# A two-layer hybrid decoder trunk on one core: products of seven blocks in both FFNs, and the order at the FFN's end

## The chip, the cores and the metric

One NeuronCore of a Trainium2 chip runs the whole program in one launch. The metric is device time in microseconds. The engines are called PE (TensorE; PEld is its weight load), DVE (VectorE), ACT (ScalarE), POOL (GpSimd) and SP (SyncE, which here only issues DMAs). DMAs are issued by SP and by POOL.

## The reference

Two layers, each a mixer and an FFN with a sandwich norm around both. The FFN is what the change is about:

```python
def ffn_sublayer(h, pre_g, post_g, w_up, conv_w, w_down):
    u = rms_norm(h, pre_g)
    z = jnp.einsum("bld,df->blf", u, w_up)          # 1024 -> 2 * 2816
    z = causal_depthwise_conv(z, conv_w)            # 3 taps
    g, up = jnp.split(z, 2, axis=-1)
    y = jnp.einsum("blf,fd->bld", jax.nn.silu(g) * up, w_down)
    return h + rms_norm(y, post_g)
```

The mixer before it joins forgetting attention (8 heads), a conv module and a short gated conv behind one input projection, norms each head and projects out. The sequence is 512 tokens and 16 meta tokens, L = 528, float32.

## The kernel before

**Precision and tiling.** Activations lie as [128 features, 528 positions] tiles. Each float32 matmul is made of three fp32r matmuls on split operands (hi x hi, hi x lo, lo x hi; `mm3`, L786). A weight chunk is loaded by SP as `raw`, rounded by ACT to `whi`, and DVE subtracts to get `wlo`. In the FFN's main loop that is `prep_one` (L591, L592 for the parts of a pair of seven; L601, L602 for whole chunks); in the stages with an order written out by hand it is `plan_block` (loads L734, ACT L738, DVE L742). `next_w` keeps two weights ahead.

**The FFN.** `w_up` has 22 gate blocks and 22 up blocks of 128 columns; pair f is gate block f and up block f. They run in three parts of 8, 7 and 7 pairs. After each part eight blocks of `w_down` are multiplied with that part's gated values: in parts 0 and 1 in the main loop, summed into `yp` (L2351, L2353), in part 2 in `finish` together with the post norm and the first products of what follows. `ffn_gate` (L2117 on) makes the gated values of a pair: three conv taps each for gate and up (ACT L2120, DVE L2122), silu (ACT L2132), the product (DVE L2136), and its split into `y` (ACT L2139, DVE L2140), which the down products read.

**Products of seven.** In layer 1 (`SEVEN_IN = (1,)`) twelve of the 22 pairs (`SEVEN`) are not made as 2 x 8 x 3 x 2 matmuls but as seven block products over half of the features and half of the positions, 7 x 4 x 3 matmuls (`seven_pair`, `product`, L2234). They need four differences of u blocks, which `normalised` builds during part 0 (DVE and ACT, in the gaps of pairs 2 to 6 and during the down products), and three parts of weights beside the gate chunk: two halves `c` and `b` of a sum of gate and up blocks, and half of the up chunk, `d`. Parts `b` are split into the tiles `shi` and `slo` (one buffer each), `d` into `y7`. During these parts h lies in DRAM (`h_dram`), and its tile serves as four more `raw` buffers.

**Weight sums.** The sum for a pair is made in DRAM ahead of its use (`sum_steps`, L525): three copies issued by SP (L537 to L539), then three accumulating DMAs issued by POOL (L533). `SUMS = {1: (8, 4)}` puts eight of layer 1's sums into layer 0's FFN and four into mixer 1. In an FFN one step is taken at each `tick`, once a pair and once a down block: POOL copies one column of a fresh result (L2152) and the step is issued behind it. In a mixer the steps are queued in the planner at the lowest urgency, one sum each `SUM_EVERY` us, each add due `SUM_LAT` us after the step before it.

**Stored splits.** During layer 0's down products, `store_one` (L610) splits six of mixer 1's weight chunks ahead (L615, L616) into `whi`/`wlo` of a pool of five buffers and POOL writes them to DRAM (L619), from where mixer 1 fetches them ready.

**Order.** Mixers, `finish` and the first products run under an order written out by a planner (`Flow`, `tc.manual_schedule`), with costs and due times given in the code; the FFN's main loop is ordered by the tile framework. `tc.issue_after(x)` makes what is issued inside come behind x on x's engine. In `finish`, `products` runs the first two down blocks with all but the last gated pair first, because the last one arrives late:

```python
for group in (ks[:-1], ks[-1:]):
    for h in range(2):
        for i in range(2):
```

so the accumulator of the first half takes k = 0 to 5 at once (f = 15 to 20 in part 2), and only f = 21 is left for the end. ACT loads the table set for the norms behind the last silu (L2135).

Of the kernel before, what the change touches and what calls it, by code (L numbers as in the profile page):

```python
# [10 lines left out]
F32 = mybir.dt.float32  # L11
F32R = mybir.dt.float32r
BF16 = mybir.dt.bfloat16
AF = mybir.ActivationFunctionType
ALU = mybir.AluOpType

P = 128
# [10 lines left out]
NF = DFF // P  # L28
# [3 lines left out]
SEVEN = (8, 9, 10, 11, 12, 13, 15, 16, 17, 18, 19, 20)  # L32
SEVEN_IN = (1,)
SUMS = {1: (8, 4)}
SUM_US, SUM_LAT, SUM_EVERY = 0.9, 5.0, 40.0
K2 = KD // 2
# [352 lines left out]
def tile_hybrid_trunk(ctx: ExitStack, tc: tile.TileContext, xT, wflat, pv_d, out):  # L389
# [135 lines left out]
    def sum_steps(l, f):  # L525

        gate, up = (flat_w(up_chunk[l, t]) for t in (f, NF + f))
        t = sums[l, f] = T(dram, [P, 4, SB], F32, f"w_sum{l}_{f}")
        n, o = P * 2 * SB, offs[up_chunk[l, f]]
        diag = wflat[o:o + 2 * (n + SB)].rearrange("(e q) -> e q", e=2)[:, :n].rearrange("e (p s) -> p e s", p=P)[:, :, :SB]  # L530

        def put(to, src):
            nc.gpsimd.dma_start(to, src, accum_op=ALU.add)  # L533

        def copies():
            with tc.issue_after(last_load[0].ins):
                nc.sync.dma_start(t[:, 0], up[:, :SB])  # L537
                nc.sync.dma_start(t[:, 1], up[:, :SB])
                nc.sync.dma_start(t[:, 2:4], gate.rearrange("p (e s) -> p e s", e=2))  # L539

        return copies, lambda: put(t[:, 0:2], diag), lambda: put(t[:, 2], t[:, 1]), lambda: put(t[:, 3], t[:, 2])

# [67 lines left out]
    def store_one():  # L610

        if fetched:
            i, sz, raw = fetched.popleft()
            hi, lo = (T(wx[0], [P, WCHUNK], F32R, t) if sz <= WCHUNK else T(wp, [P, CHUNK], F32R, t) for t in ("whi", "wlo"))
            nc.scalar.copy(hi[:, :sz], raw[:, :sz])  # L615
# [1192 lines left out]
    def finish(norms, h, h_at, spans, ks, rhs, y_at, yp, gpost, gpre, nsplit, first=None, rz=None, scaled=None,  # L1808
# [45 lines left out]
        def products():  # L1854

            m1 = KD - nsplit
            for m0, z in [(m, m + 2) for m in range(0, m1, 2)] + [(m1, KD)]:
                for hf in range(2):
# [4 lines left out]
                    if m0 == 0:  # L1863
# [6 lines left out]
                        t = [mmt(x.buf) for x in slots]  # L1870
                        for group in (ks[:-1], ks[-1:]):
                            for h in range(2):
# [170 lines left out]
    for l in range(DEPTH):  # L2043
# [23 lines left out]
        with tc.tile_pool(name=f"fp{l}", bufs=2, reuse_waits="tile") as fp:  # L2067
# [57 lines left out]
            def ffn_gate(f):  # L2125

                cs = []
                for e, t in enumerate((f, NF + f)):
                    c = T(fp, [P, 2, H], F32, "c", 4).rearrange("p a b -> p (a b)")[:, :2 * fw]
                    gate_conv(t, zs[(2 * f + e) % len(zs)], c)  # L2130
                    cs.append(c)
                silu = nc.scalar.activation(cs[0], cs[0], AF.Silu)  # L2132
                if f == NF - 1:
                    with tc.issue_after(silu.ins):
                        nc.scalar.preload_act_table_set(EXPSET)  # L2135
                mul_ins[0] = nc.vector.tensor_mul(cs[0], cs[0], cs[1])  # L2136
                slot = next(f - sum(PARTS[:p]) for p in range(len(PARTS)) if f < sum(PARTS[:p + 1]))
                ghi, glo = (t[:, :2 * fw] for t in y_pair(slot))
                nc.scalar.copy(ghi, cs[0])  # L2139
                glo_ins[0] = nc.vector.tensor_sub(glo, cs[0], ghi.bitcast(F32))  # L2140
# [5 lines left out]
            seven = SEVEN if l in SEVEN_IN else ()  # L2146
            todo = deque(step for to, place in ((l + 1, 0), (l, 2)) for f in sums_at(to, place) for step in sum_steps(to, f))

# [65 lines left out]

            mul_ins, glo_ins = [None], [None]
            ts, n_seven, primed = [], [0], set()
# [74 lines left out]
            for part, nf in enumerate(PARTS):  # L2291
# [65 lines left out]
                else:  # L2357
# [7 lines left out]
                    if not final:  # L2365
# [3 lines left out]
                        first = First(lambda b, k, hf, raw=raw: raw[hf][b][k] if raw[hf] else u_rhs(b, k, hf), [H, H], {})  # L2369
                    with tc.manual_schedule(engines=every):  # L2370
                        plan_begins()
                        norms.factors([rs, zs[0][:, 2:]], h=APART)
                        flow.yields = YE
                        if not final:
                            plan_w(after_down, WE)
                        plan_w(len(chunks) if final else after_mixer[l + 1])
                        t_last = [Tok(flow.now + 7.5)]
                        finish(norms, h, {}, o_spans, ks, grhs, lambda k, nf=nf: t_last if k == nf - 1 else [], yp,
                               gains("ffn_post_g"), gpre, SPLIT["ffn_w_down"], first, raw=raw, rzs=rzs, u_at=u_at)
# [52 lines left out]
```

## Time and profile before

| what | value |
|---|---|
| median of three runs | 1286.39 us (1286.29 to 1289.18) |
| profiled execution | 1285.76 us |
| its span, first to last instruction | 1283.8 us |
| mean granted PE clock | 0.996 |
| DMA moved, mean rate | 176.30 MB, 137 GB/s |
| mixer 0, FFN 0 (about) | 32 to 276 us, 276 to 635 us |
| mixer 1, FFN 1 (about) | 673 to 915 us, 915 to 1284 us |

How to read the profile: an engine's share is its busy time over the span. The chain of waits is followed back from the last instruction to what released each step, so its shares say which engine's work set the end. A window's row gives a stretch, its length, each engine's busy time (and instructions), the granted PE clock, the share of the 16 DMA engines and GB/s. A timeline's row gives start, duration, engine, line, what it writes and reads, and in brackets how long the engine was idle and what ended that. `x2` merges two in a row.

### The profile page before, as it was taken

What the parts mean: (1) busy time and instruction counts of PE and PEld (TensorE: products, weight loads), DVE (VectorE), ACT (ScalarE), POOL (GpSimd) and SP (SyncE); (2) the same over time, 40 slices, a digit from 0 to 9 for tenths busy, and PEclk for the clock granted to TensorE, in tenths of its full rate; (3) what the DMA queues carried; (4) which work ended last, traced back from release to release, by engine and by line L of the source; (5) the groups of instructions that cost most, each with busy time, mean ns of one, the idle gap of its engine ahead of it and who ended that gap; (6) DMA issues with size and microseconds to landing.
All of it is one profiled execution on the core that took longest, in us unless ns stands there. A gap on an engine that the chain in (4) does not pass through costs nothing.

```text
span 1283.8 us, 24209 instructions
## 1 busy us (share of the span) xinstructions
PE 1261.4 (98%) x9660; PEld 1209.3 (94%) x9660; DVE 889.3 (69%) x1505; ACT 666.9 (52%) x1273; POOL 155.1 (12%) x333
## 2 busy tenths in 40 slices
PE   8999999999999999999999999999999999999987
PEld 8999899999999999999999998999999799989987
DVE  7888765688634764566578887756799648747854
ACT  7254577564333432244573545766555457527643
POOL 1313311001122112100003234110000000000000
PEclk9999999999999999999999999999999999999989
DMA  7136132605579638732552585555134235344511
GB/s 241 34 102 160 51 101 91 224 18 149 150 230 265 168 95 243 190 105 75 172 218 63 155 192 116 137 130 181 73 120 140 92 122 181 115 140 141 199 50 67
DMA packets 69393, 176.30 MB, mean 137 GB/s; under 512 B 7632, under 2 KB 18000, under 8 KB 69024
## 3 DMA queue, kind: packets, MB, share of 16 engines
q1 hardware_dynamic: 60784, 155.74, 38.0%
q0 software_dynamic: 8496, 19.01, 8.4%
q8 instruction: 76, 1.25, 0.4%
q14 instruction: 37, 0.30, 0.1%
HBM read 151.09 MB, written 37.95 MB: 147 GB/s over the span
## 4 chain that ended last, share of the span: by engine, by line
PE 91%; DVE 4%; ACT 2%; DMA 1%; issue 1%; POOL 0%; SPq 0%; DVEq 0%; ACTq 0%
PE psum L786 68%; PE psum L2234 9%; PE psum L1356 4%; PE psum L1620 3%; PE psum L1586 2%; PE psum L923 1%; DMA raw<-in_w_dram 1%; PE psum L1542 1%; PE psum L1686 1%; PE psum L1272 1%; ACT whi L738 1%; DVE c L2122 0%; DVE wlo L742 0%; DVE yp L999 0%; POOL dm L1557 0%
## 5 line engine op out<-in xcount | busy, mean ns | idle before, releaser
L786 PE MATMUL psum<-y,whi 128*128 128x264 f32 (+3 forms) x1968 | 386.8, 300 | 7.2 <-ACT y L2139 3.7
L786 PE MATMUL psum<-uhi,whi 128*128 128x264 f32 (+1 forms) x1456 | 349.8, 288 | 1.7 <-ACT uhi L2018 0.7
L786 PE MATMUL psum<-ulo,whi 128*128 128x264 f32 (+1 forms) x1456 | 343.3, 284 | 0.6 <-DVE ulo L2020 0.4
L786 PE MATMUL psum<-uhi,wlo 128*128 128x264 f32 (+1 forms) x1456 | 342.5, 284 | 0.0
L786 PEld LDWEIGHTS psum<-y,whi 128*128 128x128 f32 x1968 | 306.5, 189 | 22.1 <-ACT y L2139 4.3
L786 PE MATMUL psum<-y,wlo 128*128 128x264 f32 (+3 forms) x984 | 273.7, 298 | 1.1 <-DVE wlo L742 1.1
L786 PEld LDWEIGHTS psum<-uhi,whi 128*128 128x128 f32 x1456 | 245.9, 188 | 6.2 <-issue 2.0
L786 PEld LDWEIGHTS psum<-ulo,whi 128*128 128x128 f32 x1456 | 246.0, 188 | 1.3 <-DVE ulo L2020 0.6
L786 PEld LDWEIGHTS psum<-uhi,wlo 128*128 128x128 f32 x1456 | 245.5, 188 | 0.0
L786 PEld LDWEIGHTS psum<-y,wlo 128*128 128x128 f32 x984 | 178.1, 189 | 6.7 <-DVE wlo L742 1.5
L601 ACT CAST whi<-raw 128x1024 fp32r<-128x1024 f32 (+1 forms) x80 | 82.2, 1029 | 116.3 <-PE psum L786 84.2
L2122 DVE SCALAR_TENSOR_TENSOR c<-zs,pv,c 128x528 f32<-128x528 f32 (+1 forms) x176 | 131.1, 756 | 10.1 <-ACT c L2120 8.1
L602 DVE TENSOR_TENSOR wlo<-raw,whi 128x1024 fp32r<-128x1024 f32 (+1 forms) x80 | 95.7, 1198 | 41.4 <-ACT whi L601 40.6
L742 DVE TENSOR_TENSOR wlo<-raw,whi 128x1024 fp32r<-128x1024 f32 (+2 forms) x80 | 95.5, 1203 | 30.2 <-ACT whi L738 29.7
L738 ACT CAST whi<-raw 128x1024 fp32r<-128x1024 f32 (+2 forms) x80 | 81.8, 1030 | 27.5 <-PE psum L786 20.2
L1102 DVE SCALAR_TENSOR_TENSOR cacc<-apad,pv,cacc 128x528 f32<-128x528 f32 x120 | 87.7, 772 | 0.1
L2139 ACT CAST y<-c 128x528 fp32r<-128x528 f32 (+1 forms) x44 | 27.5, 626 | 73.0 <-DVE c L2136 72.9
L2120 ACT ACTIVATE c<-zs,pv 128x528 f32<-128x528 f32 (+1 forms) x88 | 63.2, 727 | 3.2 <-DVE zs L2272 1.5
L2085 DVE TENSOR_TENSOR zs<-psum,rz 128x528 f32<-128x528 f32 x40 | 28.3, 708 | 51.4 <-PE psum L786 50.5
L1620 PE MATMUL psum<-pf,vals 128*128 128x400 f32 (+3 forms) x160 | 50.7, 399 | 0.6 <-POOL pf L1600 0.6
L1586 PE MATMUL psum<-q,k 128*128 128x128 f32 (+2 forms) x192 | 51.2, 348 | 0.0
L2132 ACT ACTIVATE c<-c 128x528 f32<-128x528 f32 (+1 forms) x44 | 28.1, 640 | 44.3 <-DVE c L2122 44.3
(265 smaller groups left out, 1974.3 us busy)
## 6 DMA issues: line engine op xcount, KB each, us to landing
raw<-in_w_dram SPq DMA_DIRECT2D x135, 512.0 KB, 4.2
raw<-in_w_dram SPq DMA_DIRECT2D x27, 448.0 KB, 4.2
h<-w_sum SPq DMA_DIRECT2D x14, 512.0 KB, 4.1
h<-in_w_dram SPq DMA_DIRECT2D x13, 512.0 KB, 3.7
w_sum<-in_w_dram SPq DMA_DIRECT2D x24, 256.0 KB, 8.9
w_sum<-in_w_dram SPq DMA_DIRECT2D x12, 512.0 KB, 6.9
w_sum<-in_w_dram POOLq DMA_DIRECT2D x12, 512.0 KB, 7.6
w_sum<-w_sum POOLq DMA_DIRECT2D x24, 256.0 KB, 5.4
```

The source lines that it names most:

```text
L601: nc.scalar.copy(hi[:, :sz], raw[:, :sz])
L602: nc.vector.tensor_sub(lo[:, :sz], raw[:, :sz], hi[:, :sz].bitcast(F32))
L738: nc.scalar.copy(box["hi"][:, :sz], box["raw"][:, :sz])
L742: nc.vector.tensor_sub(lo[:, :sz], box["raw"][:, :sz], box["hi"][:, :sz].bitcast(F32))
L786: nc.tensor.matmul(d, lhsT=w[a][:, k, cols], rhs=rhs(b, k, hf), start=start and i == 0 and p == 0, stop=stop and i == n - 1 and p == 2)
L1102: nc.vector.scalar_tensor_tensor(conv[j], in0=src, in1=conv[j], scalar=col("a_dw_w", CK * j + i), op0=ALU.mult, op1=ALU.add)
L1356: nc.tensor.matmul(ps[:n, :nw], lhsT=(uhi, ulo)[ui][:, k, P * b:P * b + n], rhs=w[wi][:, k % 4, :], start=k == 0 and p == 0, stop=k == KD ...
L1586: nc.tensor.matmul(s, lhsT=k[:, ka:ka + kn], rhs=q[:, s0:qz], start=i == 0, stop=i == 1)
L1620: nc.tensor.matmul(acc[:, s0 - qa:qz - qa], lhsT=vals[:, b].rearrange("p h d -> p (h d)")[:, o:o + P], rhs=box["p"], start=b == 0, stop=b ...
L2120: nc.scalar.activation(dst, src[:, 2:2 + 2 * fw], AF.Copy, scale=wtap(2, t))
L2122: nc.vector.scalar_tensor_tensor(dst, in0=src[:, i:i + 2 * fw], scalar=wtap(i, t), in1=dst, op0=ALU.mult, op1=ALU.add)
L2234: nc.tensor.matmul(psum[:, bank, :n7], lhsT=w[a][:, k0 + k, :], rhs=rhs(b, k), start=start and k == 0 and p == 0, stop=stop and k == K2 - ...
```

## The change

Six edits. (a) The products of seven are used in both layers, with their preparation and the move of h to DRAM. (b) The weight sums are spread: for layer 0 eight in mixer 0 and four in its own FFN; for layer 1 five in layer 0's FFN, six in mixer 1 and one in its own FFN; in a mixer one each 25 us instead of 40, with 9 us instead of 5 allowed for a step. The steps of the FFN's own sums come ahead of those for the next layer. A sum is entered in `sums` with its last add. (c) `store_one` splits chunks of up to 1024 columns into `shi`/`slo`. (d) In `finish` the first down blocks take the last two gated pairs one by one, with due times of 3.5 and 7.5 us. (e) The table load moves behind the rounding of the last gated pair. (f) What `finish` issues on ACT comes behind the rounding of the last but one pair.

```diff
-SEVEN_IN = (1,)
-SUMS = {1: (8, 4)}
-SUM_US, SUM_LAT, SUM_EVERY = 0.9, 5.0, 40.0
+SEVEN_IN = (0, 1)
+SUMS = {0: (0, 8, 4), 1: (5, 6, 1)}
+SUM_US, SUM_LAT, SUM_EVERY = 0.9, 9.0, 25.0
...
-        t = sums[l, f] = T(dram, [P, 4, SB], F32, f"w_sum{l}_{f}")
+        t = T(dram, [P, 4, SB], F32, f"w_sum{l}_{f}")
...
+        def last():
+            put(t[:, 3], t[:, 2])
+            sums[l, f] = t
...
-            hi, lo = (T(wx[0], [P, WCHUNK], F32R, t) if sz <= WCHUNK else T(wp, [P, CHUNK], F32R, t) for t in ("whi", "wlo"))
+            hi, lo = (T(tx[0], [P, 2 * SB], F32R, t) for t in ("shi", "slo")) if sz <= 2 * SB else (T(wp, [P, CHUNK], F32R, t) for t in ("whi", "wlo"))
...
-                        for group in (ks[:-1], ks[-1:]):
+                        for group in (ks[:-2], ks[-2:-1], ks[-1:]):
...
-                silu = nc.scalar.activation(cs[0], cs[0], AF.Silu)
-                if f == NF - 1:
-                    with tc.issue_after(silu.ins):
-                        nc.scalar.preload_act_table_set(EXPSET)
+                nc.scalar.activation(cs[0], cs[0], AF.Silu)
...
-                nc.scalar.copy(ghi, cs[0])
+                ghi_ins[f] = nc.scalar.copy(ghi, cs[0])
+                if f == NF - 1:
+                    with tc.issue_after(ghi_ins[f].ins):
+                        nc.scalar.preload_act_table_set(EXPSET)
...
-            todo = deque(step for to, place in ((l + 1, 0), (l, 2)) for f in sums_at(to, place) for step in sum_steps(to, f))
+            todo = deque(step for to, place in ((l, 2), (l + 1, 0)) for f in sums_at(to, place) for step in sum_steps(to, f))
...
-                    with tc.manual_schedule(engines=every):
+                    with tc.issue_after(ghi_ins[NF - 2].ins), tc.manual_schedule(engines=every):
...
-                        t_last = [Tok(flow.now + 7.5)]
-                        finish(norms, h, {}, o_spans, ks, grhs, lambda k, nf=nf: t_last if k == nf - 1 else [], yp,
+                        t_last = {nf - 2: [Tok(flow.now + 3.5)], nf - 1: [Tok(flow.now + 7.5)]}
+                        finish(norms, h, {}, o_spans, ks, grhs, lambda k: t_last.get(k, []), yp,
```

More of the change, by code (lines that the diff above doesn't have):

```diff
@@ L539, in copies @@
                 nc.sync.dma_start(t[:, 2:4], gate.rearrange("p (e s) -> p e s", e=2))
-        return copies, lambda: put(t[:, 0:2], diag), lambda: put(t[:, 2], t[:, 1]), lambda: put(t[:, 3], t[:, 2])
+        return copies, lambda: put(t[:, 0:2], diag), lambda: put(t[:, 2], t[:, 1]), last
     def sums_at(l, place):
@@ L2213, in normalised @@
                 ts.extend((t[:, 0], t[:, 1]) for t in tiles)
-            mul_ins, glo_ins = [None], [None]
+            mul_ins, glo_ins, ghi_ins = [None], [None], {}
             ts, n_seven, primed = [], [0], set()
```

## The prediction

> **What bounds the kernel now.** I read the page first, then the chain of waits, then windows by stage.
>
> ```profile
> span 1283.8 us, 24209 instructions
> PE 1261.4 (98%) x9660; PEld 1209.3 (94%) x9660; DVE 889.3 (69%) x1505; ACT 666.9 (52%) x1273; POOL 155.1 (12%) x333
> PE 91%; DVE 4%; ACT 2%; DMA 1%; issue 1%; POOL 0%; SPq 0%; DVEq 0%; ACTq 0%
> ```
>
> TensorE is busy 98% of the span and makes 91% of the chain that ends last. So a matmul taken away shortens the time by its cadence, as long as what feeds TensorE keeps up. The chain in order of time gives the cadence:
>
> ```profile
> 493.55 122.41 PE psum L786 x1002
> ...
> 1039.22 49.25 PE psum L2234 x408
> ...
> 1150.87 49.28 PE psum L2234 x410
> ```
>
> A 264-column matmul of layer 0's FFN comes every 122.41/1002 = 0.1222 us. The products of seven in layer 1 (258 columns) come every 0.1207 and 0.1202 us.
>
> Windows, with the columns stretch, length, PE, PEld, DVE, ACT, POOL, clock, DMA share, GB/s: layer 0's FFN (its part 0, the part's down products, part 1, and the rest), layer 1's FFN, and the two mixers.
>
> ```profile
> 276.50:370.00 93.50, 92.80 (x761) 92.59 (x760) 63.77 (x82) 41.44 (x55) 13.48 (x17) 1.00 0.51 141
> 370.00:417.00 47.00, 47.00 (x389) 47.00 (x388) 17.03 (x17) 15.50 (x20) 11.52 (x18) 1.00 0.93 273
> 417.00:488.00 71.00, 71.00 (x584) 71.00 (x584) 48.58 (x60) 28.64 (x37) 9.74 (x13) 1.00 0.53 132
> 488.00:499.00 11.00, 10.49 (x82) 9.87 (x81) 6.37 (x9) 2.42 (x3) 2.24 (x4) 1.00 0.95 282
> 499.00:540.00 41.00, 41.00 (x340) 41.00 (x339) 19.11 (x22) 11.00 (x12) 9.08 (x15) 1.00 0.83 222
> 540.00:606.00 66.00, 66.00 (x543) 66.00 (x542) 45.22 (x56) 27.51 (x35) 1.46 (x2) 1.00 0.33 98
> ...
> 920.50:1003.00 82.50, 82.30 (x646) 80.20 (x645) 70.82 (x118) 38.74 (x54) 0.00 (x0) 1.00 0.35 109
> 1003.00:1033.00 30.00, 29.03 (x126) 23.10 (x125) 15.67 (x16) 15.00 (x20) 0.00 (x0) 1.00 0.32 103
> 1033.00:1098.00 65.00, 65.00 (x517) 63.70 (x516) 47.23 (x61) 44.47 (x79) 0.00 (x0) 1.00 0.52 162
> ...
> 49.00:250.00 201.00, 199.73 (x1508) 185.64 (x1507) 143.83 (x320) 116.91 (x284) 43.39 (x105) 1.00 0.37 111
> 690.00:887.00 197.00, 195.77 (x1490) 182.27 (x1488) 144.77 (x322) 114.17 (x279) 55.86 (x117) 1.00 0.56 143
> ```
>
> Layer 0's FFN leaves TensorE idle for 1.2 us in 329.5. Layer 1's FFN already runs what the change brings to layer 0, so its rows are the twin from which most costs are taken: in 1033 to 1098 TensorE is never idle, VectorE is busy 47.23 of 65 us, ScalarE 44.47.
>
> The one place with a real wait is the end of layer 1's FFN (chain, timelines of VectorE, ScalarE and TensorE, TensorE by windows):
>
> ```profile
> 1222.60 0.68 DVE L2136 TENSOR_TENSOR c<-c,c 128x512 f32<-128x512 f32 x1
> ...
> 1222.72 1.78 ACT L738 CAST whi<-raw 128x896 fp32r<-128x896 f32 x2 [2.19 <-PE psum L786]
> 1224.66 0.94 ACT L738 CAST whi<-raw 128x896 fp32r<-128x896 f32 x1
> 1225.77 0.64 ACT L2132 ACTIVATE c<-c 128x512 f32<-128x512 f32 x1
> 1226.43 1.28 ACT L2135 ACT_TABLE_LOAD   x1
> 1227.72 0.62 ACT L2139 CAST y<-c 128x512 fp32r<-128x512 f32 x1
> 1228.25 0.72 ACT L2120 ACTIVATE c<-zs,pv 128x512 f32<-128x512 f32 x1
> 1231.30 0.62 ACT L2139 CAST y<-c 128x512 fp32r<-128x512 f32 x1 [2.33 <-DVE c L2136]
> ...
> 1228.39 0.58 PE L786 MATMUL psum<-y,whi 128*128 128x256 f32 x1 [3.72 <-ACT y L2139]
> ...
> 1239.45 17.68 PE psum L786 x147
> ...
> 1225.00:1230.00 5.00, 1.46 (x5) 0.67 0.77 250
> 1230.00:1235.00 5.00, 5.00 (x31) 0.65 0.06 25
> 1235.00:1240.00 5.00, 4.93 (x41) 1.00 0.01 3
> ```
>
> The gated product of f=20 is ready at 1222.60 + 0.68 = 1223.3, but ScalarE first splits three weights of the end, then runs f=21's silu and a table load, and rounds f=20 only at 1227.72. TensorE waits 3.72 us and then runs at 0.65 of its clock until about 1233.
>
> **The change part by part.** The sum is made against the profiled execution, 1285.76 us (1283.8 us of span and 2.0 around it); the median of the runs is 1286.39, 0.6 above.
>
> (1) Matmuls. A pair in layer 0 falls from 2 x 8 x 3 x 2 = 96 to 7 x 4 x 3 = 84. Twelve pairs save 144 x 0.1222 = 17.6 us; two priming matmuls give 0.2 back. The products' cadence at 258 columns is 0.0009 to 0.0014 us above 0.1222 x 258/264 = 0.1194; over 1008 products that is 0.9 to 1.4 us, but this scaling leaves no fixed part, so the bounds are 0 and 1.4, and I take 0.7. Together -16.7.
>
> (2) Preparing u and its four differences in part 0. The twin loses 0.2 us up to 1003 and 1.0 at the following down products; layer 0 today loses 0.7 and 0. Net +0.5 (bounds 0 and 2). VectorE has the room: 63.77 of 93.5 today, 70.82 of 82.5 in the twin.
>
> (3) The pairs' extra copies and splits: nothing, as in 1033 to 1098. Without the cover, the two engines would still be under three quarters full.
>
> (4) Loads.
>
> ```profile
> raw<-in_w_dram SPq DMA_DIRECT2D x135, 512.0 KB, 4.2
> w_sum<-in_w_dram SPq DMA_DIRECT2D x24, 256.0 KB, 8.9
> w_sum<-in_w_dram POOLq DMA_DIRECT2D x12, 512.0 KB, 7.6
> ...
> 908.14 5.78 SPq L2329 DMA_DIRECT2D h_dram<-h  x2
> ```
>
> A pair fetches 512 + 512 + 512 + 256 = 1792 KB where it fetched 1024, so 9.4 MB more in twelve pairs; h goes out and comes back, 4.3 MB; nine sums instead of eight, 2 MB. At the 297 GB/s of 282/0.95 this is 53 us of the DMA engines on top of 195 (share times length, summed over the six windows), in about 312 us: 80%. Under 0.93 TensorE stayed full (47.00 of 47), and the twin sends h away before part 0 begins to press (908), so I take 1.0; bounds 0 and 8, the upper one where the first two pairs' 3.7 MB must pass in a down stretch that is at 0.93 already and the loss falls on TensorE in part.
>
> (5) The six stored splits move from a pool of five buffers to shi/slo, one buffer, which the pairs' second piece uses too. What is queued behind such a wait on ScalarE is part 0's own copying out of PSUM.
>
> ```profile
> 388.20 0.86 POOL L533 DMA_DIRECT2D w_sum<-w_sum  x1 [1.83 <-DMA w_sum<-in_w_dram]
> 388.76 0.86 POOL L619 DMA_DIRECT2D w_split<-wlo  x1
> 395.29 0.83 POOL L533 DMA_DIRECT2D w_sum<-w_sum  x1 [5.48 <-DMA w_sum<-w_sum]
> 396.01 1.66 POOL L619 DMA_DIRECT2D w_split<-whi  x1
> ```
>
> Here one store's low half leaves at 388.76 behind an add, and the next store's high half is out 7.3 us later, so the next cast would have to wait until that DMA has landed. Nearest price: up to one us for each of six, since a down block of 42 to 48 matmuls (5 to 6 us) covers most. I take 1.5, bounds 0 and 6.
>
> (6) Layer 0's FFN gets the end that layer 1 has. With the new order the five earlier k run first on all four accumulators, 60 matmuls or 7.3 us, then f=20, then f=21: 0.5, bounds 0 and 5.8 (the whole loss of (7)).
>
> (7) Layer 1's end. The first block has 7 x 3 x 4 = 84 matmuls from 1222.75; at 17.68/147 = 0.1203 us they end at 1232.9, and with 0.77 for the copy out that stands before 1239.45 today the next block starts at 1233.6. That is 5.8 us earlier, cold clock included. f=21 is needed at 1222.75 + 72 x 0.1203 = 1231.4; without the table load and f=20's rounding ahead of it, its 1231.30 + 0.62 becomes about 1230.0. I take -5.8, bounds -6.3 and -1.3 (the table load alone).
>
> The Trainium skill, TensorE: Matmul & The Clock Gate, section "What's actually happening", has the clock halve after an idle window of about 3.4 us. The trace agrees in kind: 0.65 to 0.67 after the 3.72 us wait, 1.00 in every window above whose waits are shorter. By the page a wait just under 3.4 us at this place would already give the cold part back; the sum does not need it.
>
> (8) Mixers. Mixer 0 gets eight sums, mixer 1 six instead of four. In mixer 1 four sums took the DMA share from 0.37 to 0.56 and left TensorE idle for 1.2 us, in mixer 0 without sums it was 1.3. POOL's adds are in order with the masks of attention:
>
> ```profile
> POOL w_sum L533 <- DMA w_sum<-in_w_dram: 45.6, 7, 11.9
> POOL w_sum L533 <- DMA w_sum<-w_sum: 34.1, 7, 7.7
> ```
>
> so a late copy stops a mask; the planner now allows 9 us for a landing instead of 5, which is above the 7.6 and near the 8.9 of the rows above. I take +0.8; bounds -1 and +4. Layer 1's own sum in part 0 of its FFN: nothing, DMA is at 0.35 there.
>
> Sum: -16.7 + 0.5 + 1.0 + 1.5 + 0.5 - 5.8 + 0.8 = -18.2, so 1267.6 beside the profiled 1285.76 and 1268 beside the median.
>
> **The rivals.**
> A: both ends wait. The new order ties ScalarE to f=20's rounding alone; the three splits can still stand ahead of f=21's chain. Then layer 1's end gains the table load's 1.3 only, and layer 0's end pays 3.72 and the cold clock, 5.8 in all: 1268 + 4.5 + 5.3 = 1278. For it: three splits stand there today. Against: f=20 alone made the 3.72. By the Trainium skill's clock page, named above, the cold part comes with any such wait.
> B: DMA in layer 0's down stretches. The 8 of (4): 1268 + 7 = 1275. For it 0.93 and 0.95, against it 47.00 of 47.
> C, slower: the pieces of layer 0's pairs come late. A load that lands as the sums' copies do, in 8.9 us instead of 4.2, is 4.7 late; one block product, 12 or 24 matmuls, covers about 2.2; 2.5 in each of twelve pairs is 30: 1298. It decides from 18.2/12 = 1.5 us a pair on. For it: sums and stores share the queues there, unlike in the twin; against it: seven raw tiles in turn, and 80% is not full.
> D: the products of seven save nothing in layer 0 because something else already sets its pace: 1286. Against it 47.00 of 47, 71.00 of 71, 66.00 of 66.
>
> **How the numbers follow.** Forecast 0.70 (its own range 1261 to 1273, from the bounds that are not a rival's), A 0.09, B 0.12, C 0.07, D 0.02. The range 1260 to 1278 takes in A and B and leaves C and D out. Faster by over 0.3% (3.9 us, about what a measurement of this kernel can tell from no change) are forecast, A and B: 0.91; D is within it, 0.02; C slower, 0.07.
>
> **What would show it.** (1) 9660 matmuls become 9518, and the twelve pairs take about 84 x 0.1226 = 10.3 us each with PE full. (2) PE idle under 1.5 us up to the first down products. (4), B, C: a DMA share of 0.95 and more with gaps on PE named after raw or w_sum. (5) waits of ScalarE's shi cast for a w_split DMA. (6), (7), A: no PE wait over 1 us and a clock of 1.00 at both ends. (8) the mixers' stretches longer by under 1 us each. The prediction is wrong if layer 0's FFN shrinks by less than 10 us, or if PE at layer 1's end still waits.

## The result, and the profile after

The change makes the kernel slower: 1297.75 us median of four runs (1296.72 to 1300.88) beside 1286.6 (1286.29 to 1289.18) for the kernel before, a ratio of 1.0086 (95% interval 1.0065 to 1.0108). The profiled execution took 1298.15 us. The forecast was 1268. Line numbers of the changed kernel are four higher than before behind L533, but only one higher for the product (L2137) and the rounding of the gated values (L2140).

From the page of the changed kernel: span, busy time, two DMA queues (q1 holds what SP issues, q0 what POOL issues) and the chain by engine.

```profile
span 1296.4 us, 24290 instructions
PE 1253.3 (97%) x9518; PEld 1198.9 (92%) x9518; DVE 915.8 (71%) x1561; ACT 716.1 (55%) x1389; POOL 195.9 (15%) x377
q1 hardware_dynamic: 73360, 182.09, 43.3%
q0 software_dynamic: 15216, 31.59, 15.5%
PE 82%; DMA 8%; DVE 4%; ACT 3%; issue 2%; POOL 1%; SPq 1%; DVEq 0%; ACTq 0%; POOLq 0%
```

The 142 matmuls are gone and TensorE is busy 8.1 us less, but the span is 12.6 us longer: TensorE's idle time has grown from 22.4 to 43.1 us, and DMA's share of the chain from 1% to 8%. Where, shows when the two traces are laid over each other at the same matmuls (start of the last norm matmul of mixer 0's sublayer, of one at layer 0's FFN end, of the last head norm of mixer 1, and the end):

| stage, us | before | after | difference |
|---|---|---|---|
| mixer 0 | 259.8 | 269.8 | +10.0 |
| FFN 0 | 388.3 | 387.8 | -0.5 |
| mixer 1 | 206.7 | 215.0 | +8.3 |
| out-projection 1 and FFN 1 | 429.0 | 423.8 | -5.2 |
| span | 1283.8 | 1296.4 | +12.6 |

Windows of the changed kernel, columns as in the prediction: mixer 0, part 0's pairs, the start of its down products, their rest, part 1, the start of its down products, their rest, part 2, mixer 1, and FFN 1's end.

```profile
49.00:259.00 210.00, 202.38 (x1501) 187.42 (x1500) 143.14 (x318) 116.27 (x283) 66.72 (x129) 0.98 0.73 177
286.50:362.00 75.50, 75.50 (x620) 75.50 (x619) 64.64 (x96) 36.69 (x50) 8.93 (x12) 1.00 0.62 172
362.00:382.00 20.00, 13.49 (x106) 12.87 (x105) 11.80 (x14) 8.06 (x11) 2.94 (x6) 0.90 0.68 216
382.00:426.00 44.00, 43.04 (x342) 42.69 (x343) 18.33 (x19) 18.12 (x27) 11.17 (x17) 0.97 0.81 196
426.00:498.00 72.00, 70.85 (x580) 70.42 (x580) 56.17 (x75) 48.63 (x86) 9.13 (x12) 1.00 0.75 213
498.00:518.00 20.00, 15.08 (x102) 14.12 (x101) 9.81 (x13) 6.75 (x9) 3.82 (x6) 0.83 0.76 251
518.00:551.00 33.00, 33.00 (x273) 32.93 (x272) 12.97 (x15) 9.71 (x14) 7.81 (x13) 1.00 0.85 248
551.00:617.00 66.00, 66.00 (x546) 66.00 (x545) 52.18 (x71) 46.13 (x83) 8.21 (x12) 1.00 0.75 202
700.00:905.00 205.00, 198.82 (x1487) 184.99 (x1486) 144.30 (x320) 114.06 (x279) 62.85 (x128) 0.98 0.63 157
...
1230.00:1235.00 5.00, 5.00 (x44) 5.00 (x43) 3.56 (x6) 3.01 (x6) 0.00 (x0) 1.00 0.25 98
1235.00:1240.00 5.00, 5.00 (x44) 5.00 (x43) 2.67 (x5) 1.71 (x3) 0.00 (x0) 1.00 0.31 95
```

The pairs of seven themselves keep TensorE full (75.50 of 75.50, 66.00 of 66, 70.85 of 72). FFN 0 loses mainly at two places, where the down products of parts 0 and 1 begin: 6.5 and 4.9 us of 20 idle, with the clock at 0.90 and 0.83. FFN 1's end runs at full clock without a wait. The mixers are idle for 7.6 and 6.2 us where they were idle for 1.3 and 1.2, at a DMA share of 0.73 and 0.63 instead of 0.37 and 0.56.

The chain in order of time (start, length, what) names the transfers that TensorE waits for in mixer 0:

```profile
75.85 4.88 DMA k<-sq
...
107.98 5.81 DMA k<-pair_hi
...
229.15 6.71 DMA raw<-in_w_dram
```

The DMA issues of mixer 0 (60 to 255 us) before, KB each and median us to landing, give the times to set beside them:

```profile
raw<-in_w_dram SPq DMA_DIRECT2D x27, 512.0 KB, 4.2
k<-pair_hi SPq DMA_DIRECT2D x12, 132.0 KB, 2.4
k<-sq SPq DMA_DIRECT2D x8, 2.1 KB, 1.6
```

In these stretches no weight sum stands on the chain itself: small transfers of attention, one of 2.1 KB among them, and the loads of the out-projection land later, 4.9 for 1.6 us, 5.8 for 2.4 and 6.7 for 4.2.

And for FFN 0, the chain at the two stops:

```profile
364.28 6.68 DMA w_split<-slo
...
371.04 1.24 DVE slo L620
...
372.29 6.80 DMA raw<-in_w_dram
...
379.18 0.07 ACT shi L619
...
380.13 1.04 ACT whi L605
381.18 0.51 ACT yp L2355
...
488.75 14.33 DMA w_split<-shi
...
503.11 1.04 ACT shi L619
504.15 0.65 ACT c L2124
```

The stored splits set both. In part 0 the subtraction of one (L620) waits until the one before has landed, only then a raw buffer is free for the next load, and the rounding of that load (L619) waits for it on ScalarE. Behind it stand the rounding of the third down block's weight (L605) and the copy of the first down block out of PSUM (L2355); TensorE has finished the first two blocks at 375.58 and stands until 381.72. At 488.75 a store's landing takes 14.33 us; ScalarE's timeline shows what waits with it:

```profile
494.39 0.93 ACT L605 CAST whi<-raw 128x896 fp32r<-128x896 f32 x1
495.23 0.64 ACT L2321 COPY zs<-psum 128x264 f32<-128x264 f32 x2
503.11 1.04 ACT L619 CAST shi<-raw 128x1024 fp32r<-128x1024 f32 x1 [7.24 <-DMA w_split<-shi]
504.06 0.73 ACT L2124 ACTIVATE c<-zs,pv 128x528 f32<-128x528 f32 x1
504.70 0.63 ACT L2136 ACTIVATE c<-c 128x528 f32<-128x528 f32 x1
505.23 0.62 ACT L2140 CAST y<-c 128x528 fp32r<-128x528 f32 x1
508.80 0.63 ACT L2140 CAST y<-c 128x528 fp32r<-128x528 f32 x1 [2.96 <-DVE c L2137]
```

ScalarE stands still for 7.24 us at the rounding of a chunk that only mixer 1 needs, over 150 us later. Behind it in its queue are the rounding of pair 13 (505.23; its product was ready at 498.3) and a tap, the silu and the rounding (508.80) of pair 14, on which the down products wait: TensorE stands for 4.32 us until 505.90.

### The profile page after: what moved, and what is told of

It reads as the page before. It is cut to its first block, busy times and chain, and to the rows that moved or that the text cites. A ratio compares the mean times of both kernels' runs of the same rounds, so it can differ in the third digit from the quotient of the medians.

```text
span 1296.4 us, 24290 instructions
## 1 busy us (share of the span) xinstructions
PE 1253.3 (97%) x9518; PEld 1198.9 (92%) x9518; DVE 915.8 (71%) x1561; ACT 716.1 (55%) x1389; POOL 195.9 (15%) x377
## 4 chain that ended last, share of the span: by engine, by line
PE 82%; DMA 8%; DVE 4%; ACT 3%; issue 2%; POOL 1%; SPq 1%; DVEq 0%; ACTq 0%; POOLq 0%
PE psum L790 51%; PE psum L2238 17%; PE psum L1360 4%; DMA raw<-in_w_dram 4%; PE psum L1624 3%; PE psum L1590 2%; PE psum L927 2%; DMA w_split<-shi 1%; PE psum L1546 1%; DMA k<-pair_hi 1%; DMA k<-sq 1%; DMA w_sum<-in_w_dram 1%; PE psum L1690 1%; PE psum L1276 1%; DMA w_split<-slo 1%
## 5 line engine op out<-in xcount | busy, mean ns | idle before, releaser
L790 PE MATMUL psum<-uhi,whi 128*128 128x264 f32 (+1 forms) x1072 | 273.2, 290 | 1.8 <-ACT uhi L2022 0.8
L790 PE MATMUL psum<-ulo,whi 128*128 128x264 f32 (+1 forms) x1072 | 267.2, 285 | 0.6 <-DVE ulo L2024 0.4
L790 PE MATMUL psum<-uhi,wlo 128*128 128x264 f32 (+1 forms) x1072 | 266.4, 285 | 0.0
L790 PEld LDWEIGHTS psum<-uhi,whi 128*128 128x128 f32 x1072 | 188.1, 190 | 6.3 <-issue 2.0
L790 PEld LDWEIGHTS psum<-ulo,whi 128*128 128x128 f32 x1072 | 188.1, 190 | 1.3 <-DVE ulo L2024 0.6
L790 PEld LDWEIGHTS psum<-uhi,wlo 128*128 128x128 f32 x1072 | 187.8, 190 | 0.0
L605 ACT CAST whi<-raw 128x1024 fp32r<-128x1024 f32 (+1 forms) x51 | 52.5, 1029 | 71.1 <-PE psum L790 49.1
L2238 PE MATMUL psum<-uhi,whi 128*128 128x264 f32 (+1 forms) x288 | 81.8, 285 | 1.7 <-ACT acc L2268 1.0
L2238 PE MATMUL psum<-ulo,whi 128*128 128x264 f32 (+1 forms) x288 | 81.4, 283 | 0.0
L2238 PE MATMUL psum<-uhi,wlo 128*128 128x264 f32 (+1 forms) x288 | 80.8, 283 | 0.0
L606 DVE TENSOR_TENSOR wlo<-raw,whi 128x1024 fp32r<-128x1024 f32 (+1 forms) x51 | 61.0, 1196 | 25.0 <-ACT whi L605 24.8
L2238 PE MATMUL psum<-t,shi 128*128 128x264 f32 (+1 forms) x384 | 72.4, 283 | 0.4 <-ACT shi L595 0.4
L2238 PEld LDWEIGHTS psum<-t,shi 128*128 128x128 f32 x384 | 59.4, 189 | 0.7 <-ACT shi L595 0.7
```

Of the source, the lines that this page charges most:

```text
L606: nc.vector.tensor_sub(lo[:, :sz], raw[:, :sz], hi[:, :sz].bitcast(F32))
L790: nc.tensor.matmul(d, lhsT=w[a][:, k, cols], rhs=rhs(b, k, hf), start=start and i == 0 and p == 0, stop=stop and i == n - 1 and p == 2)
L2238: nc.tensor.matmul(psum[:, bank, :n7], lhsT=w[a][:, k0 + k, :], rhs=rhs(b, k), start=start and k == 0 and p == 0, stop=stop and k == K2 - ...
```

## The experiments

Two things were to be settled: what makes the mixers slower (the order on SP's queue, or the load of the sums on the DMA engines), and what the stored splits cost in FFN 0 and why. All stages in us, cut at the same matmuls as above; the time is the median where there were several runs.

| run | us | mixer 0 | FFN 0 | mixer 1 | rest | what differs |
|---|---|---|---|---|---|---|
| before | 1286.6 | 259.8 | 388.3 | 206.7 | 429.0 | |
| after | 1297.75 | 269.8 | 387.8 | 215.0 | 423.8 | |
| e1 | 1290.21 | 259.6 | 388.7 | 210.4 | 429.6 | before, a sum each 25 us |
| e2 | 1312.19 | 283.6 | 388.0 | 215.2 | 422.5 | after, the mixers' copies issued by POOL |
| e8 | 1280.02 | 262.4 | 385.4 | 207.8 | 422.4 | after, no adds in the mixers |
| e6 | 1281.54 | 261.6 | 387.1 | 207.6 | 422.5 | after, light sums |
| e3 | 1283.97 | 273.3 | 368.7 | 209.4 | 430.8 | after, nothing stored |
| e5 | 1270.3 | 261.7 | 368.9 | 209.0 | 430.9 | light sums, nothing stored |
| e4 | 1295.53 | 271.1 | 388.0 | 212.6 | 422.0 | after, stores in `whi`/`wlo` |
| e9 | 1308.8 | 261.7 | 402.3 | 209.1 | 433.9 | light, stores in two quarters of h |
| e10 | 1282.3 | 260.4 | 390.2 | 207.9 | 422.1 | light, two store buffers in h, three raw |
| e11 | 1279.07 | 261.8 | 384.4 | 207.8 | 422.7 | light, stores issued by ScalarE |
| e15 | 1280.66 | 261.6 | 379.6 | 206.8 | 430.9 | light, loaded and split, not written |
| e12 | 1282.59 | 271.2 | 375.9 | 213.5 | 422.0 | after, stores behind the last gated pair |
| e13 | 1269.53 | 260.9 | 375.9 | 208.1 | 422.1 | light, the same placing |
| e14 | 1291.82 | 261.0 | 396.9 | 206.7 | 424.0 | light, stores behind their down block |
| e16 | 1263.84 | 261.5 | 374.2 | 208.9 | 422.1 | e13, two blocks earlier |
| e17 | 1263.53 | 261.8 | 370.1 | 206.9 | 423.7 | e16, issued by ScalarE |
| e7 | 1279.57 | 259.8 | 388.5 | 206.7 | 422.6 | before, the new end alone |

In e3, e5 and e15 mixer 1 splits all its weights itself, and the same cuts hold 9 matmuls fewer in FFN 0 and 37 fewer in mixer 1 than in the other changed kernels, and 46 more in the rest. At 0.122 us each, 1.1 us of what these three gain in FFN 0 is work that has moved behind the cut. Most runs give one profile, and the stages are as good as one execution: after, e3, e4 and e12, which have the same mixer 0, differ there by up to 3.5 us.

### The mixers

**e1: the closer spacing, with its longer step time, in the kernel before.** Mixer 1 keeps four sums.

```diff
-SUM_US, SUM_LAT, SUM_EVERY = 0.9, 5.0, 40.0
+SUM_US, SUM_LAT, SUM_EVERY = 0.9, 9.0, 25.0
```

> The kernel before with the sums of mixer 1 (still four) 25 us apart instead of 40 and 9 us allowed for a step instead of 5. Theory 1 (place): in the changed kernel both mixers stop where the second and the third sum's copies stand on SP just ahead of the small transfers of k; 25 us puts them there, 40 did not. Then mixer 1 loses about 8 us here at the same two places (3.9 and 4.3), total 1294. Rival (number): it is how many sums a mixer carries; with four as before it loses 0 to 1 us, total 1286 to 1287.

Mixer 1 takes 210.4 us instead of 206.7: four sums at the new spacing cost 3.7, about half of what the changed kernel loses there with six. That lies between what the two theories expected.

**e2: the copies off SP's queue.** If the copies stood in front of attention's own transfers on SP, issuing them from POOL would free these.

```diff
-                nc.sync.dma_start(t[:, 0], up[:, :SB])
+                q.dma_start(t[:, 0], up[:, :SB])
...
-            tok = flow.op("sp", 2.0, copies, (Tok(flow.pe + SUM_EVERY * i),), prio=8, lat=SUM_LAT)
+            tok = flow.op("pool", 3 * SUM_US, copies, (Tok(flow.pe + SUM_EVERY * i),), prio=8, lat=SUM_LAT)
```

> The changed kernel with the three copies of each sum in a mixer issued by POOL instead of SP. Theory 1a (order on SP's queue): the small k transfers no longer stand behind 1 MB; the two stops in each mixer (1.4 + 4.4 and 3.9 + 4.3 us) go and the mixers gain 6 to 8 us each, less up to 2 us for POOL's extra work: total 1284 to 1288. Rival (shared DMA engines): the 16 engines are the same, the stops stay within 1 us: 1296 to 1299.

It went the other way: mixer 0 grows from 269.8 to 283.6. The same 2.1 KB transfer at the same place of the chain now takes

```profile
76.36 7.05 DMA k<-sq
```

So the order on SP's queue is not what delays it, and neither theory had allowed for a loss of 14 us. The out-projection's loads are later as well (one takes 15.52 us, chain at 234.72). Mixer 1 does not change (215.2 for 215.0), and why the copies cost more from POOL stays open. The Trainium skill, DMA: Bandwidth & Descriptors, section "Issuing engines are not separate DMA queues", says that DMAs of all issuers share the same 16 engines and that spreading them saves issue time alone; mixer 0 agrees that nothing was gained, and shows a loss besides.

**e8: the copies without the adds.** The three accumulating DMAs of each mixer sum are left out, so those sums hold the bare copies.

```diff
-            for op in adds:
-                tok = gp(SUM_US, op, tok, prio=8, lat=SUM_LAT)
+            gp(SUM_US, lambda l=l, f=f: sums.update({(l, f): sums_t[l, f]}), tok, prio=8, lat=SUM_LAT)
```

> The changed kernel with the three accumulating DMAs of each mixer's sum left out, so that the sums stay unfinished copies (the output is then not the reference's); the copies stay where they are. If the copies are what is late for (theory 1), the stops before k in the mixers stay: mixers 6 to 10 us over before each, total 1293 to 1298. If the adds or POOL's waits for them are (rival), the mixers fall back to 0 to 3 us each: total 1281 to 1287.

Mixer 0 falls to 262.4 and mixer 1 to 207.8: the adds make 7.4 of the 10.0 and 7.2 of the 8.3 us. They do not act through POOL's order: TensorE's waits for the masks that POOL makes behind them are 0.3 us for `dm` in the changed kernel's mixer 0, and 0.4 before. The queues of mixer 0 (60 to 255 us; packets, MB, share of 16 engines) suggest why so few bytes weigh so much. Changed kernel:

```profile
q1 hardware_dynamic: 12287, 27.78, 44.5%
q0 software_dynamic: 4327, 8.12, 31.5%
```

Here q0 is the adds alone. They move 8.12 MB in 0.315 x 195 = 61.4 us of all 16 engines, 132 GB/s; everything else goes at 27.78 MB / (0.445 x 195 us) = 320 GB/s. That the adds delay the small transfers by the engine time they take is read from these shares; no run tests it by itself.

**e6: fewer and slower sums in the mixers.** Four in each, one each 40 us; the rest goes into the FFNs. The runs called light have this.

```diff
-SUMS = {0: (0, 8, 4), 1: (5, 6, 1)}
-SUM_US, SUM_LAT, SUM_EVERY = 0.9, 9.0, 25.0
+SUMS = {0: (0, 4, 8), 1: (1, 4, 7)}
+SUM_US, SUM_LAT, SUM_EVERY = 0.9, 5.0, 40.0
```

> The changed kernel with the stored splits as they are, and the sums placed as in the run above (four in each mixer, 40 us apart). Theory: the mixers, 10 and 8 us longer in the changed kernel, fall back to 0 to 2 us each, layer 0's FFN stays at its 388 us: total 1280 to 1284. Rival (the mixers' loss comes from elsewhere, the order or the FFN's prefetch): mixers stay 5 or more over before, total 1290 or more.

Of the 18.3 us that the two mixers lose, 2.7 are left (261.6 and 207.6), and FFN 0 and FFN 1 don't suffer from the sums moved into them (387.1 and 422.5).

### The stored splits

**e3 and e5: nothing stored ahead.** Mixer 1 splits its weights itself, as it does with all others.

```diff
-MASK = "111111000000000000000000"
+MASK = "000000000000000000000000"
```

> The changed kernel without the stored splits of mixer 1's six weight chunks: mixer 1 loads and splits them itself, as mixer 0 does. Theory 2 (the stores are what stops PE at the first down blocks of parts 0 and 1, about 7 and 8 us with the cold clock): layer 0's FFN is 13 to 15 us shorter, mixer 1 up to 3 us longer: total 1283 to 1288. Rival (weights come late in those stretches for other reasons, the pairs' pieces and the sums): FFN gains under 5 us, total 1293 to 1300.

> The changed kernel without stored splits and with the sums moved out of the mixers: four in each mixer, 40 us apart with 5 us for a step as the kernel before has them, eight of layer 0's in its own FFN, seven of layer 1's in its own FFN. Theory (three separate causes): layer 0's FFN keeps the 19 us that the run without stores gained over both kernels, layer 1's end its 5, and the mixers fall back to 0 to 2 us over before each: total 1262 to 1268. Rival (any sum in a mixer or any denser FFN costs again): FFN 0 or FFN 1 gives back 5 or more, total 1270 to 1280.

Without them FFN 0 takes 368.7 and 368.9 us: 19.1 less than in the changed kernel and 18.2 less than beside the light sums. Without the 1.1 us of moved matmuls the stored splits cost 18.0 and 17.1. Both stops are gone (the like window of e3: 19.55 of 20 busy). In exchange mixer 1 and the rest are longer by 1.4 + 8.4 = 9.8 (e5 against e6), 8.7 without the moved matmuls, so what the stores do for the mixer is worth half of what they cost. e5, four runs: 1270.3 us (1268.07 to 1272.28), ratio 0.9866 (0.9849 to 0.9882).

**e4, e9, e10: other buffers.** In e4 the splits go into the three buffers of `whi`/`wlo`; in e9 into two quarters of h, which leaves two fewer for raw; in e10 into all four in turn as two pairs, with three raw buffers until the last store.

```diff
-            hi, lo = (T(tx[0], [P, 2 * SB], F32R, t) for t in ("shi", "slo")) if sz <= 2 * SB else (T(wp, [P, CHUNK], F32R, t) for t in ("whi", "wlo"))
+            hi, lo = (T(wp, [P, CHUNK], F32R, t) for t in ("whi", "wlo"))
...
+            hi, lo = (spare[0][:, 2 * j:2 * j + 2, :].rearrange("p a b -> p (a b)").bitcast(F32R) for j in (2, 3))
```

The first new line is e4's, the second e9's; e10's takes the pairs (2, 3) and (0, 1) in turn.

> The changed kernel with the stored splits made in the weight ring whi/wlo (three buffers) instead of shi/slo (one): the same DMAs, another buffer. Theory 2a (the single buffer, which waits for the DMA out of the last store): layer 0's FFN gains 10 to 15 us as without stores, total 1283 to 1289. Rival 2b (DMA share of the stretch): gain under 3 us, total 1295 to 1299. If the ring itself is then short of a buffer, the waits go to the weights' casts (L605) instead and the gain is between.

> Light sums (four in each mixer, 40 us apart) with the stored splits made in two free quarters of h's tile, which lies in DRAM meanwhile: one buffer pair for the stores alone, no longer that of the pairs' second piece, and five raw tiles in turn instead of seven. The DMAs are the same as in the run with light sums. If the sharing with the pairs' piece is what stops PE at the first down blocks, layer 0's FFN falls from 387 to 370 to 376 us, total 1264 to 1271. If it is store after store in one buffer, each waiting for the last one's DMA out (7 to 14 us), it gains under 6 us: total 1276 to 1281.

> The same with two pairs of buffers for the stores (all four quarters of h's tile in turn) and only three raw tiles until the stores are done. Theory (a store waits for the DMA out of the store before): the waits at the first down blocks go, layer 0's FFN 370 to 376 us, total 1264 to 1271. Rival (DMA share of that stretch): FFN stays over 380, total 1275 to 1281; the same if three raw tiles are too few for the pairs, then with waits for raw in the pairs of part 1.

None helps: 388.0, 402.3 and 390.2. The waits move to what gave up its buffer. In e4 the chain in part 1's pairs reads

```profile
409.23 5.85 DMA raw<-w_sum
...
417.39 8.76 DMA w_split<-whi
```

and e9 still stops for the landing of a store in front of part 1's down products. e9's last stage is 12 us longer than e10's: its edit leaves layer 1's FFN five raw buffers instead of seven too, and TensorE is idle there for 11.9 us instead of 4.7, the difference mostly in waits for rounded weights.

**e11: the stores' DMAs issued by ScalarE**, so that they don't stand in line with the adds on POOL.

```diff
-                nc.gpsimd.dma_start(stored[i][:, n], t[:, :sz].bitcast(F32))
+                nc.scalar.dma_start(stored[i][:, n], t[:, :sz].bitcast(F32))
```

> Light sums with shi/slo as in the changed kernel, but the stores' DMAs issued by ACT instead of POOL. If the landing of 7 to 14 us comes from POOL's queue (an add ahead of it, POOL waiting for an add's source), landing falls to 4 to 7 us and layer 0's FFN gains 5 to 12 us: total 1270 to 1277. If it is the 16 DMA engines' load, landing and FFN stay: total 1279 to 1283.

FFN 0 384.4 instead of 387.1: the second stop is shorter, the first stays.

**e15: loaded and split, but not written.** The light sums; the three lines of `store_one` that write to DRAM are left out.

> The light sums; the six chunks are still loaded and split during layer 0's down blocks, but not written to DRAM, and mixer 1 splits them for itself. It tells the waits for the stores' landing from the load of raw buffers, ScalarE and VectorE. Theory (the waits are for the landing of the stores): layer 0's FFN 367 to 372 us, as without any stored split (368.9), whole 1270 to 1274. Rival (raw buffers and loads): FFN 378 to 388 us, whole 1280 to 1290.

FFN 0 takes 379.6, 10.7 more than without any stored split at the same cuts: of the 17.1 us the writes make only 6.4, so the landing of the stores alone is not the cause. The chain at part 1's down products:

```profile
478.98 12.47 DMA raw<-in_w_dram
...
491.47 1.05 ACT shi L619
```

The rounding now waits 6.6 us for its own load, which takes 12.47, at the same place of ScalarE's queue. That points to the place: whatever this instruction waits for, pair 14 waits behind it.

**e12 and e13: the place alone.** The stored splits are issued behind the rounding of the part's last gated pair, in the changed kernel (e12) and beside the light sums (e13).

```diff
                             if l == 0 and m % 2:
-                                store_one()
+                                with tc.issue_after(ghi_ins[f0 + nf - 1].ins):
+                                    store_one()
```

> The changed kernel, with the six stored splits placed on ScalarE and VectorE behind the rounding of the part's last gated pair (and nothing else changed). In the changed kernel's trace three stored roundings (shi) stand on ScalarE ahead of the first down block's weight, and one ahead of the silu of pair 14; each waits for the store before it to land. Theory (place in ScalarE's queue): the waits still last as long, but nothing that TensorE needs at the start of the down blocks is behind them; layer 0's FFN falls from 387.8 to 370 to 376 us and the whole to 1280 to 1287. Rival (DMA load, or the raw buffers that the stored chunks hold): the stall only moves into the pairs of parts 1 and 2, FFN 383 to 390 us, whole 1293 to 1300.

> The same placing in the kernel with the light sums (4 sums in each mixer, one each 40 us). Theory (place in the queue): layer 0's FFN from 387.1 to 370 to 376 us, mixer 1 keeps what the stored splits give it, whole 1264 to 1271. Rival (DMA load or raw buffers): whole 1278 to 1284.

FFN 0 falls from 387.8 to 375.9 and from 387.1 to 375.9 with the same loads, splits, writes and buffers. Windows of e12 over the two places:

```profile
362.00:382.00 20.00, 19.55 (x161) 19.33 (x160) 15.59 (x20) 10.32 (x14) 3.83 (x6) 1.00 0.62 181
486.00:506.00 20.00, 19.69 (x162) 19.48 (x161) 12.37 (x16) 9.57 (x14) 3.84 (x6) 1.00 0.98 245
```

Both stops are gone, the second at a DMA share of 0.98. The chip's time follows: e12 1282.59 us (1279.11 to 1284.96), ratio 0.9962 to the kernel before (0.9948 to 0.9975), e13 1269.53 (1265.48 to 1271.27), ratio 0.986 (0.9837 to 0.9884). FFN 0 still has 7.0 us over the kernel without stores, 5.9 without the moved matmuls. 2.2 of them are a stop that ends at 410.17 in e13, whose chain names a weight sum, not a store: POOL's column copy stands behind an add that waits for its copies.

```profile
397.69 9.93 DMA w_sum<-in_w_dram
...
407.91 0.85 POOL w_sum L533
408.75 0.19 POOL cols L2156
```

**e14: too late is worse.** Each stored split comes behind the copy out of its down block.

```diff
-                                store_one()
+                                with tc.issue_after(out_ins):
+                                    store_one()
```

> The light sums, each stored split placed behind the copy out of the down block that it follows in the program (on ScalarE in part 0, on VectorE in part 1) instead of the last gated pair's rounding. Theory (place in the queue): in part 0 as good as the placing behind the gated pair or better; in part 1 only VectorE is held, ScalarE's roundings may still go ahead, so the gap of about 4.6 us at the start of part 1's down blocks stays: whole 1268 to 1276. Rival (DMA load or raw buffers): 1278 to 1284.

It lost more than either theory allowed: FFN 0 396.9, and 1291.82 us. ScalarE's timeline:

```profile
402.04 1.05 ACT L619 CAST shi<-raw 128x1024 fp32r<-128x1024 f32 x1
...
415.87 1.04 ACT L595 CAST shi<-raw 128x1024 fp32r<-128x1024 f32 x1 [6.57 <-issue]
```

The last split of part 0 takes `shi` at 402.04, when part 1's first pair of seven has begun; that pair's second piece gets the buffer 13.8 us later, and TensorE stands for 9.6 us (and for 8.1 once more at 534).

**e16 and e17: earlier, and no chunk left lying.** As e13, with the stores behind blocks 1, 3 and 5, and no chunk fetched at a part's last one, so that none occupies a raw buffer through part 1's pairs. e17 adds the edit of e11.

```diff
-                            if l == 0 and m % 2:
+                            if l == 0 and m in (0, 1, 3, 5):
                                 with tc.issue_after(ghi_ins[f0 + nf - 1].ins):
-                                    store_one()
+                                    store_one(m < 5)
...
-    def store_one():
+    def store_one(more):
...
-        if to_store:
+        if to_store and more:
```

> As e13, with the stores of a part two down blocks earlier (after blocks 1, 3 and 5 instead of 3, 5 and 7, and after 1) and no stored chunk left lying in a raw buffer through the pairs of part 1. In e13 layer 0's FFN still loses 7.0 us against the kernel without stored splits (375.9 against 368.9), 3.6 of it as gaps at 407 and 440 in part 1's first pairs. Theory (their shi waits for the last store of part 0, and one of three raw buffers is held): FFN 369 to 373 us, whole 1263 to 1267. Rival (load of the DMA engines): FFN 374 to 378, whole 1267 to 1271.

> As e16, the stores' DMAs issued by ScalarE instead of POOL, where they stand in line with the weight sums' adds. Issued by ScalarE alone (e11) it took 2.5 us off. Theory (a store's landing is late because its issue stands behind adds): another 1 to 3 us off e16. Rival (with the place put right nothing waits for the store): the same as e16 within 1 us.

1263.84 us (1261.5 to 1268.73) and 1263.53 (1262.48 to 1264.46): both 24 us below the kernel before (1287.58 beside them), ratios 0.9818 (0.9794 to 0.9843) and 0.9808 (0.9792 to 0.9825). In the profile of e17 FFN 0 is within 1.2 us of the kernel without stored splits, 1.1 of which are the moved matmuls, and mixer 1 has their benefit. The medians don't part the two, so the rival holds for e17 as far as they show: with the place put right, the issue is worth nothing that is clear of noise. (e16's profiled run was its slowest, 1268.73; its 374.2 has a stop of 1.94 us at 408.6 like e13's, which e17's profile lacks. Whether e16's faster runs have it isn't known.)

### The end of layer 1's FFN

**e7: edits (d), (e) and (f) in the kernel before.**

```diff
-                        for group in (ks[:-1], ks[-1:]):
+                        for group in (ks[:-2], ks[-2:-1], ks[-1:]):
...
-                    with tc.manual_schedule(engines=every):
+                    with tc.issue_after(ghi_ins[NF - 2].ins), tc.manual_schedule(engines=every):
```

> The kernel before with only the order of the FFN's end (last two gated pairs one by one, table load behind the last rounding, ACT of the end behind the last but one rounding). Theory: the wait of 3.72 us and the cold clock at the end of layer 1's FFN go, 5 to 6 us; layer 0's end, which had no wait, stays within 0.5: total 1280.5 to 1282. Rival: the end of layer 1 is only as good in the changed kernel because its DMA and splits fall elsewhere; gain 1 to 2 us, 1285.

The last stage falls by 6.4 us, FFN 0 stays (388.5). The window that ran at 0.65 before reads

```profile
1230.00:1235.00 5.00, 4.93 (x42) 4.73 (x41) 2.82 (x5) 2.29 (x5) 0.00 (x0) 1.00 0.66 222
```

## Why the prediction was wrong, and where it was right

The differences of the stage table add up to +12.6 us of span, where the sum was -18.2. Step by step:

- **(1) to (4) and (6) were right, and rather too cautious.** Together they were put at -16.7 + 0.5 + 0 + 1.0 + 0.5 = -14.7 in FFN 0; where the stored splits are out of the way it shrinks by 18.2 (e17, the same cuts; 19.4 in e5, with the nine matmuls moved). The 142 matmuls make 17.4 of it. Preparing u, the extra copies, the loads and the end of layer 0's FFN cost nothing that shows.
- **(7) was right:** -5.8 forecast, -5.2 in the changed kernel, -6.4 alone (e7). Rival A is out.
- **(5) failed:** +1.5, bounds 0 and 6, for the stored splits in `shi`/`slo`; they cost 18.0. The wait that it looked for is there (7.24 us for w_split), and in part 0 the copying out of PSUM does stand behind it. What failed is the cover, "a down block of 42 to 48 matmuls (5 to 6 us) covers most". In part 0 the roundings wait one after another, the third until 379.18, and hold up the third block's weight besides; the two blocks that TensorE had ready end before it, and it stands for 6.14 us. In part 1 the step overlooked that a split's rounding stands ahead of the last two pairs' values, without which no down block can end: 4.32 us more, and half the clock behind both stops. e12 shows it: the place alone gives back 11.9 of the 18.0. What is left is gone in e17, beside the light sums, where the stores also come earlier, hold no raw buffer through part 1 and are issued by ScalarE; how much each of the three gives is open.
- **(8) failed:** +0.8, bounds -1 and +4; the mixers lose 18.3. The step took mixer 1 with four sums as its measure and asked only whether the adds come late for the masks. It left out the closer spacing, which costs 3.7 us at four sums (e1). The only price of a sum's bytes, in (4), was 297 GB/s; the adds go at 132. What comes late are attention's small transfers and the out-projection's loads, not the masks. e8 gives 14.6 of the 18.3 to the adds, on one profile.
- **Rival C** had the time, 1298, by luck and another way: the pieces of layer 0's pairs were to come late. TensorE is full in part 2's pairs and idle for 1.15 of 72 us in part 1's window, not for 2.5 in each of twelve pairs. B and D are out by the same rows and e5.
- Of what was to show it, "layer 0's FFN shrinks by less than 10 us" held (0.5), and the waits of ScalarE's `shi` cast for a w_split DMA, named for (5), were the right thing to look for.

The kernel before shows the place of (5) already. At the start of part 1's down products its chain reads

```profile
478.40 6.44 DMA raw<-in_w_dram
...
484.87 1.06 ACT whi L615
...
491.18 1.51 PE psum L786 x8
```

L615 is the stored split's rounding, and TensorE's gap before 491.18 is 0.13 us: the same order was there and its wait was just covered, so the prediction could have read from it what stands behind a stored split.

## What to carry to other kernels

An instruction that waits is priced by what stands behind it in its engine's real order, and at what moment: the same stored splits stop nothing at the down products when they stand behind the last gated pair, stop TensorE for 6.1 and 4.3 us ahead of it, with half the clock behind, and for 9.6 us where one holds the next pair's buffer. Price accumulating DMAs by the engine time that their queue shows, not by their bytes alone, and look at the smallest transfers on the critical chain, not at the mean share. Work that is moved ahead to save time elsewhere (here the stored splits, worth 8.7 us) should be taken out once after a change around it, to see whether it still pays.

## What the runs showed of the hardware

**Adds in DRAM.** By the time that their packets took, the accumulating DMAs of 256 and 512 KB move their bytes at 132 GB/s where the other queue, with loads, copies and transfers inside the core, reaches 320 in the same stretch. Beside them a 2.1 KB transfer took 4.88 us, and 7.05 in e2 with the copies on POOL too, where the median of eight was 1.6 without sums.

**Waits well below 3.72 us can halve TensorE's clock.** The prediction took from its windows that shorter waits than 3.72 us leave the clock at 1.00. Windows of e12 (clock in the third column from the end):

```profile
448.00:450.00 2.00, 0.55 (x5) 0.33 (x3) 0.00 (x0) 1.06 (x2) 0.00 (x0) 1.00 0.97 210
450.00:452.00 2.00, 1.53 (x9) 1.32 (x9) 1.99 (x2) 2.00 (x3) 0.00 (x0) 0.91 0.29 49
452.00:454.00 2.00, 2.00 (x11) 2.00 (x11) 1.91 (x4) 1.91 (x5) 0.00 (x0) 0.50 0.53 152
```

TensorE is idle for 1.9 us in four (two gaps, 1.48 and 0.44), and then runs at half the clock. In e13 one gap of 2.23 us does the same (0.50 in 412 to 414); in e12 one of 1.44 at 418 does not (1.00 in 420 to 425). The Trainium skill, TensorE: Matmul & The Clock Gate, section "What's actually happening", asks for an idle window of about 3.4 us, on a window that runs freely; if that means a window without any matmul, these two cases don't agree. The 0.65 that the prediction reads behind the wait of 3.72 us is a mean: from 1228 to 1233 us the clock is 0.50. So a stop of 4 to 6 us costs more than its length: in e6, with one of 4.96 us that ends at 372.47, only 74 matmuls start between 366 and 383 us, which take 9.0 us at the cadence of 0.122, so the stop cost about 8.
